# Storing half of one late output tile of a batched q·kᵀ through a second DMA queue (Trainium2, one core)

## The chip, the cores and the metric

The kernel runs on one core of a Trainium2 chip. The metric is device time in microseconds, here the median of three runs. Five engines run side by side: TensorE (PE), VectorE (DVE), ScalarE (ACT), GpSimd (POOL) and SyncE (SP). Copies between the chip's large memory and the cores' own memory are made by 16 DMA engines, which take their orders from queues; SP, ACT and POOL can each put copies on a queue of their own.

## The reference

Eight batches of twelve heads: for each of the 96 heads the 1024 x 1024 matrix of all dot products of a row of q with a row of k, in float32.

```python
batch, n_heads, seq, head_dim = 8, 12, 1024, 64
def reference(q, k):
    return np.einsum('bhid,bhjd->bhij', q, k).astype(np.float32)
```

The inputs are 25 MB each and the output is 403 MB.

## The kernel before, in words

The heads are worked on in blocks of 2, 2, 4, 8, 8 and then six times 12. For each block q and k are loaded as float32, cast to float16 by GpSimd (`cast_rows` L97, `cast_quads` L127), and transposed, by TensorE for the first two blocks (`transpose_rows` L151, L154) and by VectorE for the others (`transpose_quads` L145). The loads of a later block are issued from the ACT queue while an earlier block is being computed, the casts two blocks ahead, and the transposes one block ahead. The last loads are issued at about 734 us and the last cast begins at 831 us; after that the casts and loads are over and what is left is products and stores.

`scores` (L156 to L189) makes one head. TensorE fills a PSUM tile of two row groups with four products of 512 columns (L171), ScalarE copies the tile to a quarter of `o_sb` (L181), and this four times over. `o_sb` is one of three output buffers of 4 MB (`out_pool`, `bufs=3`): partition p holds the eight output rows 8p to 8p+7, 32 KB, which lie side by side in the output as well. When the four copies are done, SP issues one DMA of the whole head (L185), 128 partitions of 32 KB. So the copy of head n has to wait until the store of head n-3 has landed.

Everything is issued in program order (`pin`). SP's queue holds nothing but loads of the start and then the 96 stores in the order of the heads, each behind a wait for ScalarE's last copy. ACT's queue holds the loads. GpSimd issues no DMA. At the end (L304) SP waits until every DMA has landed.

Of the kernel before, what the change touches and what calls it, by code (L numbers as in the profile page):

```python
# [10 lines left out]
P = 128  # L11

@with_exitstack
def kernel(
# [6 lines left out]
    nc = tc.nc  # L21
# [3 lines left out]
    BH = B * H  # L25
# [5 lines left out]
    of = out.rearrange("b h i j -> (b h) i j")  # L31
# [4 lines left out]
    NMAX = max(sizes)  # L36
    CHUNK = 48 * 32

    consts = ctx.enter_context(tc.tile_pool(name="consts", bufs=1))
    ident = consts.tile([P, P], F16)  # L40

# [3 lines left out]
    out_pool = ctx.enter_context(tc.tile_pool(name="out_pool", bufs=3))  # L45

    pin = tc.keep_in_program_order

    def half_tile():
        half_sb = half_pool.tile([P, CHUNK], F16, tag="half")  # L50
        return half_sb

    class Block:
# [102 lines left out]
        def scores(self, n, side, ps_pool, w):  # L156

            half, g = divmod(n, self.N // 2)
            cs = slice(half * D, (half + 1) * D)

            qT = self.qT.rearrange("c (g m t) -> c g t m", t=NT, m=P)
            kT = self.kT.rearrange("c (g j) -> c g j", j=S)
            o_sb = out_pool.tile([P, NT, S], F32, tag="out")
            for u in range(NT // w):
                ps = ps_pool.tile([P, w * S], F32, tag="po")
                for tt in range(w):
                    for j in range(2):
                        js = slice(j * 512, (j + 1) * 512)
                        at = tt * S + j * 512
                        pin(  # L170
                            nc.tensor.matmul(  # L171
                                ps[:, at : at + 512],
                                qT[cs, g, w * u + tt],
                                kT[cs, g, js],
                            )
                        )
                dst = o_sb[:, w * u : w * u + w].rearrange("p t j -> p (t j)")
                if w == 1 and u % 2:
                    pin(nc.vector.tensor_copy(out=dst, in_=ps))  # L179
                else:  # L180
                    pin(nc.scalar.copy(out=dst, in_=ps))  # L181
                for do in side.get(u, []):
                    do()
            pin(
                nc.sync.dma_start(  # L185
                    out=of[self.first + n].rearrange("(p t) j -> p (t j)", p=P),
                    in_=o_sb.rearrange("p t j -> p (t j)"),
                )
            )  # L189

    blocks, first = [], 0
    for i, N in enumerate(sizes):
# [116 lines left out]
```

## Time and profile before

| what | value |
|---|---|
| median of three runs | 1063.12 us (1062.84 to 1063.62) |
| span of the profiled execution | 1061.8 us |
| what lies around it (median less span) | 1.3 us |
| busy: PE, ACT, DVE, POOL | 701.3, 697.6, 471.5, 368.3 us |
| stores on SP's queue q1 | 14688 packets, 406.85 MB, 89.1% of the 16 engines' span |
| loads on ACT's queue q10 | 2880 packets, 46.14 MB, 10.4% |
| mean DMA rate | 427 GB/s |
| issue of the last store, its landing | 1039.4 us, 1060.9 us |

The span runs from the first to the last instruction on the chip; the DMA share is the mean busy share of the 16 DMA engines, so that a share of 0.06 is one engine at work and fifteen idle. q1 includes the loads that SP issues at the start. The last twelve slices of the page show VectorE and GpSimd going idle one after the other, while the DMA row stays at 9 up to the last slice, which has a 7.

### The profile page before, as it was taken

The page shows a single profiled execution, that of the slowest core. Times are in us where ns is not written, and L with a number is a line of the kernel's source. Part 1 is how long each engine was busy: PE and PEld are TensorE (multiplying, and loading weights), DVE is VectorE, ACT ScalarE, POOL GpSimd, SP SyncE. Part 2 cuts the span into 40 slices and gives each one's busy share as a digit, 9 for nine tenths or more (in the row PEclk, how much of TensorE's full clock was granted, in tenths as well). Part 3 has the DMA queues.
Part 4 walks back from the last instruction along what each step waited for, and adds up shares of the span by engine and source line. Part 5 has one row for each costly group of instructions (what it writes and reads, how often), then busy time and mean ns, then how long its engine had stood idle before and what let it go on. Part 6 is the DMA issues. An engine that isn't in the chain of part 4 may idle for free.

```text
span 1061.8 us, 4282 instructions
## 1 busy us (share of the span) xinstructions
PE 701.3 (66%) x1568; PEld 241.6 (23%) x1568; DVE 471.5 (44%) x75; ACT 697.6 (66%) x386; POOL 368.3 (35%) x286
## 2 busy tenths in 40 slices
PE   6866755755677367773677836777367777778770
PEld 2322211211222122221222212222122222222220
DVE  2999601991696007960079600795007950000000
ACT  4856745755777366774677746777467777777771
POOL 6959128607630463303733046330463200000000
DMA  9999999999999999999999999999999999999997
GB/s 385 428 429 435 433 431 435 435 422 440 428 430 432 432 430 432 435 422 429 431 433 431 415 436 431 433 435 422 428 434 435 434 432 432 434 433 427 434 431 311
DMA packets 17588, 453.25 MB, mean 427 GB/s; under 512 B 1952, under 2 KB 1952, under 8 KB 2976
## 3 DMA queue, kind: packets, MB, share of 16 engines
q1 hardware_dynamic: 14688, 406.85, 89.1%
q10 hardware_dynamic: 2880, 46.14, 10.4%
q8 instruction: 12, 0.20, 0.1%
q14 instruction: 8, 0.07, 0.0%
HBM read 50.33 MB, written 402.65 MB: 427 GB/s over the span
## 4 chain that ended last, share of the span: by engine, by line
DMA 70%; ACT 17%; PE 7%; DVE 2%; issue 1%; POOL 1%; ACTq 0%; SPq 0%
DMA out_dram<-o_sb 70%; ACT o_sb L181 17%; PE ps L171 7%; DVE qT L145 1%; DVE kT L145 1%; DMA early<-in_q_dram 0%; POOL half_sb L127 0%; PE ps L151 0%; POOL half_sb L97 0%; DVE kT L154 0%; DVE o_sb L179 0%; ACTq L181 0%; ACT kT L154 0%; SPq L84 0%; ACTq L73 0%
## 5 line engine op out<-in xcount | busy, mean ns | idle before, releaser
L181 ACT COPY o_sb<-ps 128x2048 f32<-128x2048 f32 (+1 forms) x384 | 695.3, 1860 | 334.7 <-DMA out_dram<-o_sb 298.4
L171 PE MATMUL ps<-kT,qT 64*128 64x512 f16 x1536 | 697.2, 617 | 329.4 <-ACT o_sb L181 325.6
L127 POOL CAST half_sb<-x_sb 32x1536 f16<-32x1536 f32 (+1 forms) x256 | 346.5, 1353 | 455.1 <-DMA x_sb<-in_q_dram 318.3
L171 PEld LDWEIGHTS <-qT 64*128 64x128 f16 x1536 | 238.4, 157 | 786.3 <-issue 781.9
L145 DVE STREAM_TRANSPOSE qT<-half_sb 128x1536 f16<-128x1536 f16 (+1 forms) x34 | 232.8, 7140 | 372.2 <-issue 372.2
L145 DVE STREAM_TRANSPOSE kT<-half_sb 128x1536 f16<-128x1536 f16 (+1 forms) x34 | 234.2, 7181 | 0.0
L127 POOL CAST half_sb<-early 32x1024 f16<-32x1024 f32 x16 | 16.5, 1033 | 4.0 <-DMA early<-in_q_dram 3.3
L151 PE MATMUL ps<-ident,half_sb 128*128 128x128 f16 x32 | 4.1, 309 | 6.7 <-POOL half_sb L97 6.1
L154 DVE COPY qT<-ps 128x1024 f16<-128x1024 f16 x2 | 2.4, 1224 | 12.3 <-PE ps L151 12.3
L179 DVE COPY o_sb<-ps 128x1024 f32<-128x1024 f32 x4 | 4.9, 1224 | 4.3 <-PE ps L171 4.3
L97 POOL CAST half_sb<-early 128x512 f16<-128x512 f32 x8 | 4.6, 613 | 4.1 <-DMA early<-in_q_dram 4.1
L151 PEld LDWEIGHTS <-half_sb 128*128 128x128 f16 x32 | 3.2, 139 | 8.6 <-POOL half_sb L97 6.5
L154 ACT ACT_TABLE_LOAD x1 | 1.3, 1283 | 5.8 <-DMA early<-in_q_dram 5.8
L154 DVE COPY kT<-ps 128x1024 f16<-128x1024 f16 x1 | 1.2, 1224 | 4.3 <-PE ps L151 4.3
L154 ACT COPY kT<-ps 128x1024 f16<-128x1024 f16 x1 | 1.0, 1012 | 1.2 <-PE ps L151 1.2
masks.py:199 POOL TENSOR_SCALAR_AFFINE_SELECT ident<-ident 128x128 f16<-128x128 f16 x1 | 0.3, 292 | 0.1
masks.py:197 POOL MEMSET ident<- 128x128 f16 x1 | 0.2, 204 | 0.3 <-POOLq L293 0.3
L293 POOL MEMSET const-float32-0.0<- 128x1 f32 x1 | 0.1, 98 | 0.2 <-issue 0.2
L293 POOL MEMSET const-uint8-127<- 128x1 uint8 x1 | 0.1, 101 | 0.0
L293 POOL MEMSET const-bfloat16-1.0<- 128x1 bf16 x1 | 0.1, 100 | 0.0
L293 POOL MEMSET const-float32-1.0<- 128x1 f32 x1 | 0.1, 98 | 0.0
## 6 DMA issues: line engine op xcount, KB each, us to landing
out_dram<-o_sb SPq DMA_DIRECT2D x96, 4096.0 KB, 21.8
x_sb<-in_q_dram ACTq DMA_DIRECT2D x6, 3072.0 KB, 22.8
x_sb<-in_k_dram ACTq DMA_DIRECT2D x6, 3072.0 KB, 39.6
x_sb<-in_k_dram ACTq DMA_DIRECT2D x2, 2048.0 KB, 22.2
x_sb<-in_q_dram SPq DMA_DIRECT2D x1, 2048.0 KB, 18.0
x_sb<-in_q_dram ACTq DMA_DIRECT2D x1, 2048.0 KB, 19.0
early<-in_k_dram ACTq DMA_DIRECT2D x4, 256.0 KB, 5.0
early<-in_q_dram SPq DMA_DIRECT2D x4, 256.0 KB, 4.7
```

What stands on the lines that cost most here:

```text
L97: nc.gpsimd.tensor_copy(out=self.rows[x][:, :, half], in_=self.raw[x][:, half * n : (half + 1) * n].rearrange("p (r d) -> p r d", d=D),)
L127: nc.gpsimd.tensor_copy(out=half_sb[q0 : q0 + 32].rearrange("p (r d) -> p r d", d=32), in_=raw[32 * b : 32 * b + 32, c * m : (c + 1) * m, h],)
L145: pin(nc.vector.transpose(out=dst, in_=src))
L151: pin(nc.tensor.transpose(t_ps[:, t], self.rows[x][:, t], ident))
L154: pin(copy(out=dst, in_=src))
L171: nc.tensor.matmul(ps[:, at : at + 512], qT[cs, g, w * u + tt], kT[cs, g, js],)
L179: pin(nc.vector.tensor_copy(out=dst, in_=ps))
L181: pin(nc.scalar.copy(out=dst, in_=ps))
L293: nc = _bacc.Bacc("TRN2", target_bir_lowering=False, num_devices=1)
```

## The change

One head, the third from the end (head 93 of 0 to 95), is stored by four DMAs instead of one; the other 95 heads go as before. Each partition's eight rows are seen as two times two pairs of rows (a, b, t). The second pair of each four (b = 1) is stored by SP for all 128 partitions. The first pair of each four (b = 0) is stored by GpSimd for partitions 120 to 124 in one DMA, then by GpSimd for partitions 0 to 119 in a second one, and by SP for partitions 125 to 127. Every piece that is contiguous on both sides is 8 KB instead of 32 KB. The order of the issues in the program is: GpSimd 5, GpSimd 120, SP 128, SP 3. GpSimd's first issue waits for ScalarE's first three copies of the head by count (the fourth quarter holds rows 6 and 7, which are b = 1), and SP's for all four.

```diff
+    SPLIT = BH - 3
+    MOST = 120
+    SOME = MOST + 5
...
+    def store(eng, dst, src):
+        pin(eng.dma_start(out=dst, in_=src))
+
+    def store_head(head, dst, src):
+        if head != SPLIT:
+            store(
+                nc.sync,
+                dst.rearrange("p t j -> p (t j)"),
+                src.rearrange("p t j -> p (t j)"),
+            )
+            return
+        dst = dst.rearrange("p (a b t) j -> p a b (t j)", a=2, b=2)
+        src = src.rearrange("p (a b t) j -> p a b (t j)", a=2, b=2)
+
+        def part(eng, rows, b):
+            store(eng, dst[rows, :, b], src[rows, :, b])
+
+        part(nc.gpsimd, slice(MOST, SOME), 0)
+        part(nc.gpsimd, slice(0, MOST), 0)
+        part(nc.sync, slice(0, P), 1)
+        part(nc.sync, slice(SOME, P), 0)
...
-            pin(
-                nc.sync.dma_start(
-                    out=of[self.first + n].rearrange("(p t) j -> p (t j)", p=P),
-                    in_=o_sb.rearrange("p t j -> p (t j)"),
-                )
-            )
+            dst = of[self.first + n].rearrange("(p t) j -> p t j", p=P)
+            store_head(self.first + n, dst, o_sb)
```

## The prediction

> **What bounds the kernel now.** First the page: which resource is full, and when it stops being full.
>
> ```profile
> DMA  9999999999999999999999999999999999999997
> ...
> HBM read 50.33 MB, written 402.65 MB: 427 GB/s over the span
> ...
> DMA out_dram<-o_sb 70%; ACT o_sb L181 17%; PE ps L171 7%; DVE qT L145 1%; DVE kT L145 1%; DMA early<-in_q_dram 0%; POOL half_sb L127 0%; PE ps L151 0%; POOL half_sb L97 0%; DVE kT L154 0%; DVE o_sb L179 0%; ACTq L181 0%; ACT kT L154 0%; SPq L84 0%; ACTq L73 0%
> ...
> out_dram<-o_sb SPq DMA_DIRECT2D x96, 4096.0 KB, 21.8
> ```
>
> The DMA engines are full in every slice but the last, and the chain that ended last is mostly stores. Moving 453 MB cannot become cheaper by this change; only the last slice, where the engines are not full, can. So second, the stretches at the end (stretch, its length, busy time of the five engines, granted clock, DMA share, GB/s):
>
> ```profile
> 1050.00:1052.00 2.00, 0.00 (x0) 0.00 (x0) 0.00 (x0) 0.00 (x0) 0.00 (x0) 1.00 1.10 475
> 1052.00:1054.00 2.00, 0.00 (x0) 0.00 (x0) 0.00 (x0) 0.00 (x0) 0.00 (x0) 1.00 0.76 328
> 1054.00:1055.00 1.00, 0.00 (x0) 0.00 (x0) 0.00 (x0) 0.00 (x0) 0.00 (x0) 1.00 0.38 164
> 1055.00:1056.00 1.00, 0.00 (x0) 0.00 (x0) 0.00 (x0) 0.00 (x0) 0.00 (x0) 1.00 0.15 66
> 1056.00:1057.00 1.00, 0.00 (x0) 0.00 (x0) 0.00 (x0) 0.00 (x0) 0.00 (x0) 1.00 0.08 33
> 1057.00:1058.00 1.00, 0.00 (x0) 0.00 (x0) 0.00 (x0) 0.00 (x0) 0.00 (x0) 1.00 0.08 33
> 1058.00:1059.00 1.00, 0.00 (x0) 0.00 (x0) 0.00 (x0) 0.00 (x0) 0.00 (x0) 1.00 0.00 0
> 1059.00:1060.00 1.00, 0.00 (x0) 0.00 (x0) 0.00 (x0) 0.00 (x0) 0.00 (x0) 1.00 0.08 33
> ```
>
> A packet is counted where it starts. 33 GB/s in 1 us is one packet of 32 KB; it takes 1.213 us, which is 0.08 of sixteen engines for that us. From 1056 us on packets start one behind the other: **one engine alone works**, for about four packets, while fifteen are done. Nobody computes any more. Third, the packet and completion records of the trace, sorted by store. Each store is eight 32 KB packets and one increment on each of the 16 engines. The sixteen increments of the last store arrive, before the last one at 1060.9 us, by 8.0, 6.8, 6.5, 6.4, 6.3, 6.3, 6.3, 6.2, 5.9, 5.7, 5.6, 5.0, 4.7, 4.6 and 3.8 us. The gap between last and last but one is 0.3 us at the store that lands at 92 us, 2.3 at 460, 3.0 at 734 and 3.8 at the end: followed packet by packet, it is one engine whose packets take 1.213 to 1.231 us where the others' take 1.213, so 9.8 us for a store against 9.7. It sets the pace of the whole run and ends last. Fourth, the chain in order of time (start, us, what), and SP's own waits (total, times, longest):
>
> ```profile
> 1010.02 21.76 DMA out_dram<-o_sb
> ...
> 1031.88 1.87 ACT o_sb L181
> ```
>
> ```profile
> SPq L304 <- DMA out_dram<-o_sb: 21.0, 1, 21.0
> ```
>
> Three output buffers turn: head 95 (the last) may be written when head 92's store has landed at 1031.8, is copied by 1039.3 and issued at 1039.4. SP then waits 21.0 us for that store, until the late engine is done. That wait is all that the change can shorten.
>
> **The change, part by part.** Only head 93 (third from the end) is stored otherwise; its third copy ends at 1018.0 us, which frees GpSimd's part, and the fourth at 1019.8, which frees SP's.
>
> *Bytes on the engines.* Before, every engine moves 8 x 32 KB of head 93. After, half of it goes as before over all 128 partitions, as 16 packets of 8 KB to an engine. The other half is 120 + 5 + 3 partitions of 16 KB. At 8 partitions to an engine 120 is fifteen shares, so one engine gets none: it saves half a head, 4 x 1.213 = 4.85 us. The eight partitions left over go, one each, to up to five engines and to up to three: 2 packets of 8 KB = 2 x 0.309 = 0.62 us each (the 8 KB row is the instruction fetch, 0.309 us; 16 KB loads take 0.611), so 0, 0.62 or 1.24 us more on an engine. 8 KB packets instead of 32 KB: 0.309 x 4 = 1.236 against 1.213, 0.02 x 8 = 0.2 us on an engine at most. I take 0.1; nothing excludes a gain of 0.1, since later packets of the run vary between 1.213 and 1.23 anyway.
>
> *If the spared engine is the late one* it ends 4.85 earlier, or 4.85 - 0.62 = 4.2 if it has one of the five or three partitions: 1056.0 to 1056.7. Then the next in line is late. Last but one was at 1060.9 - 3.8 = 1057.1, the three before it at 1056.3, 1056.2 and 1055.9; with 0 to 1.24 more these end at 1057.1 to 1058.3, at 1057.5 at most, and so on. Eight extra shares lie on at most eight of the fifteen, so the engine at 1057.1 more likely has none; the others' worst is 1057.5. I take 1057.3 and 0.1 for small packets: 1057.4, that is **3.5 us** less (2.4 to 4.0).
>
> *The two GpSimd issues.* GpSimd's last cast ends at 832 us and it has nothing queued behind: its wait for ScalarE's third copy of head 93 holds up nobody. The trace shows no GpSimd issue. Bounds: 0.33 us (SP's store) to 1.26 us (the longest ACT load issue), below nothing excluded because it is a new instruction. Taken: 1 us each, hidden, since the transfer has until about 1056 us, 38 us after the third copy. If that cover were gone the part would land last, below.
>
> *SP's queue.* Two issues instead of one for head 93, 0.33 us each by the row, at most 1.26. Behind them stands head 94's issue at 1029.6; 9.8 us are free. Nothing.
>
> *Moving ahead.* A second queue means that GpSimd's half does not wait behind heads 91 and 92 on SP's queue. On fifteen engines up to 4.85 us of it may go ahead of head 92's packets; those engines were 4 to 8 us ahead of the late one, so head 92 still lands with the late one at 1031.8, at worst 4.85 later. Head 95 is then issued by 1044.3; the late engine would reach it at 1051.2 before. Cover 11.8 us from 1039.4, so nothing.
>
> *End.* SP waits on two more semaphores. The queue's rows show 0.2 to 0.4 us for such steps after the last landing: 0, since these two are up long before; at most 0.4.
>
> Sum on the profiled execution: 1061.8 - 3.5 = 1058.3. The median of the runs is 1063.12, 1.3 us above this span; taken over to the runs, 1063.1 - 3.5 = **1059.6 us**, 0.33% less.
>
> Which engine is spared decides all, and no view numbers the engines. [...] No trace here shows the numbers.
>
> **The rivals.**
>
> *Miss.* The engine left out is one of the fifteen punctual ones. Then the late engine keeps its half head and may get 0.62 or 1.24 us more, +0.1 for packets: 1060.9 + 0.1 to 1.3, in runs 1063.2 to 1064.4, **1063.6**. For it: nothing in the profile ties the late engine to the one left out; a blind draw would hit once in sixteen. Against: lateness belongs to one engine in all 96 stores, and a split by fixed counts leaves out a fixed engine, so it is hit in every run or in none, and the odds are those of a match of two fixed things. [...]
>
> *Not what it says.* GpSimd's 120 partitions are spread over all 16 engines evenly. The late engine then saves a sixteenth of half a head, 0.3 us: 1062.9 to 1063.4, within 0.2%.
>
> *Slower: head 95 waits for its buffer.* With two queues in flight stores took longer: the longest landing is 36.6 us against the median 21.8, 14.8 more, where loads stood on a second queue. If GpSimd's half delayed head 92 so, it would land at 1046.6, head 95 would be issued at 1054.2, past the 1051.2 where the late engine runs dry, and end 3 us later than before plus 1 to 2 us of start: 1066 to 1068, **1067**. It decides from a delay of 11.8 us. Against: those loads were 6 MB, GpSimd's part is 2 MB, 4.6 us at 432 GB/s.
>
> **How the numbers follow.** Hit 0.55, miss 0.34, evenly spread 0.04, slower by the buffer 0.07. The chance of a hit is a judgement: the sizes come from the trace, the match of the two engines does not; it is where I am least sure. Forecast 1059.6 with its own range 1059.0 to 1060.8. From 1058.8 to 1064.6 hit, miss and even spread are held, 0.9. A measurement of this kernel tells about 0.2% (2.1 us) from no change. Faster by more: the hit less its weakest end, 0.54. Within: 0.39. Slower: 0.07.
>
> **What would show it.** Right: in the last 6 us no stretch with one engine alone over 2 us; SP's last wait shorter than 21.0 by about 3.5; last landing near 1057.4; one engine with 4 packets of 32 KB less in the tail, and it is the late one. Miss: the row of single packets still there up to 1060 us or later, and the gap before the last increment 3 us or more. Slower: ScalarE's wait for the landing of head 92 longer than 2.3 us. Wrong sizes: 8 KB packets well over 0.31 us, or another engine made late by GpSimd's queue.

## The result, and the profile after

| | median us | runs | ratio to before, 95% interval |
|---|---|---|---|
| before, beside it | 1063.37 | 1062.84 to 1063.95 | |
| after | 1068.45 | 1068.12 to 1070.21 | 1.0053 [1.0038, 1.0067] |

The change makes the kernel 0.53% slower, about 5 us, where the prediction had 3.5 us less. The profiled execution after took 1068.75 us with a span of 1066.8 us, 5.0 more than the 1061.8 of before.

The page of after, first the two DMA rows of the slices, then the queues, the GpSimd line and the issues (out<-in, engine, count, KB each, median us from issue to landing):

```profile
DMA  9999999999999999999999999999999999999997
GB/s 378 431 432 434 432 426 430 432 431 431 434 433 424 430 435 430 434 426 431 432 431 432 424 432 433 432 432 426 429 435 432 432 434 432 431 434 431 429 354 314
...
q1 hardware_dynamic: 14825, 404.81, 88.5%
...
q0 software_dynamic: 320, 2.05, 0.7%
...
L54 POOL DMA_DIRECT2D out_dram<-o_sb x2 | 1.4, 714 | 186.2 <-ACT o_sb L207 186.2
...
out_dram<-o_sb SPq DMA_DIRECT2D x1, 2048.0 KB, 26.5
out_dram<-o_sb POOLq DMA_DIRECT2D x1, 1920.0 KB, 26.7
```

The row under the DMA row in the page of before:

```profile
GB/s 385 428 429 435 433 431 435 435 422 440 428 430 432 432 430 432 435 422 429 431 433 431 415 436 431 433 435 422 428 434 435 434 432 432 434 433 427 434 431 311
```

The DMA row reads as before: 9 in every slice but the last. The row under it doesn't: the last slice but one (1013 to 1040 us) moves 354 GB/s, where it moved 431 before and the ten slices ahead of it in after move 429 to 435. So the engines count as busy and carry less. The queue rows say the same: q0, GpSimd's, moves 2.05 MB of q1's 404.81, that is 0.51%, and takes 0.7% of the engines' span against q1's 88.5%, that is 0.79% of it.

The stretches of 4 us show where the 5 us go (stretch, length, busy time of the five engines, granted clock, DMA share, GB/s). First after:

```profile
1022.00:1026.00 4.00, 2.52 (x6) 0.94 (x6) 0.00 (x0) 3.82 (x3) 0.00 (x0) 1.00 1.02 354
1026.00:1030.00 4.00, 3.81 (x10) 1.39 (x9) 0.00 (x0) 3.02 (x2) 0.00 (x0) 1.00 0.98 307
1030.00:1034.00 4.00, 0.93 (x3) 0.20 (x2) 0.00 (x0) 0.00 (x0) 0.00 (x0) 1.00 0.93 283
1034.00:1038.00 4.00, 1.00 (x3) 0.46 (x3) 0.00 (x0) 2.92 (x2) 0.00 (x0) 1.00 0.99 311
1038.00:1042.00 4.00, 2.63 (x7) 0.63 (x4) 0.00 (x0) 3.82 (x3) 0.00 (x0) 1.00 1.05 371
```

The same stretches before:

```profile
1022.00:1026.00 4.00, 1.99 (x5) 0.78 (x5) 0.00 (x0) 3.73 (x3) 0.00 (x0) 1.00 1.01 434
1026.00:1030.00 4.00, 3.82 (x10) 1.27 (x9) 0.00 (x0) 3.56 (x2) 0.00 (x0) 1.00 1.03 442
1030.00:1034.00 4.00, 1.68 (x5) 0.62 (x4) 0.00 (x0) 2.12 (x2) 0.00 (x0) 1.00 0.99 426
1034.00:1038.00 4.00, 3.43 (x8) 0.95 (x6) 0.00 (x0) 3.83 (x3) 0.00 (x0) 1.00 1.03 442
1038.00:1042.00 4.00, 0.00 (x0) 0.00 (x0) 0.00 (x0) 1.33 (x1) 0.00 (x0) 1.00 0.93 401
```

The last column is the one to read. With a full rate of 432 GB/s (the mean from 940 to 980 us before, at a share of 1.00) the five stretches of after fall short by 78, 125, 149, 121 and 61 GB/s, 534 together; times 4 us and divided by 432 that is **4.9 us** of full transfer lost. The same sum for before is 0.1 us. So nearly the whole difference arises in these 20 us, while head 93's two halves are on the engines, at a share near 1.0 throughout. It is neither an idle engine nor one late engine: many packets take longer. By the packet records the 8 KB packets of GpSimd's queue take 458 ns in the mean and those of SP's queue 402, where 309 had been expected. Most still take about 309; 107 of GpSimd's 250 and 73 of SP's 262 take more than 330 ns, up to 2.4 us.

The tail of after, the stretches of 1 us:

```profile
1060.00:1061.00 1.00, 0.00 (x0) 0.00 (x0) 0.00 (x0) 0.00 (x0) 0.00 (x0) 1.00 0.23 98
1061.00:1062.00 1.00, 0.00 (x0) 0.00 (x0) 0.00 (x0) 0.00 (x0) 0.00 (x0) 1.00 0.23 98
1062.00:1063.00 1.00, 0.00 (x0) 0.00 (x0) 0.00 (x0) 0.00 (x0) 0.00 (x0) 1.00 0.08 33
1063.00:1064.00 1.00, 0.00 (x0) 0.00 (x0) 0.00 (x0) 0.00 (x0) 0.00 (x0) 1.00 0.08 33
```

The last increment comes at 1065.1, the one before 1.7 us earlier (3.8 before), the next 2.4. The part with one engine alone is shorter, as the forecast wanted, but it comes 5 us later. SP's last wait, in its list of waits, is accordingly longer and not shorter:

```profile
SPq L326 <- DMA out_dram<-o_sb: 22.2, 1, 22.2
```

### The profile page after: what moved, and what is told of

It reads as the page before. It is cut to its first block, busy times and chain, and to the rows that moved or that the text cites. A ratio compares the mean times of both kernels' runs of the same rounds, so it can differ in the third digit from the quotient of the medians.

```text
span 1066.8 us, 4286 instructions
## 1 busy us (share of the span) xinstructions
PE 701.0 (66%) x1568; PEld 241.6 (23%) x1568; DVE 471.5 (44%) x75; ACT 697.3 (65%) x386; POOL 369.8 (35%) x288
## 3 DMA queue, kind: packets, MB, share of 16 engines
q1 hardware_dynamic: 14825, 404.81, 88.5%
q0 software_dynamic: 320, 2.05, 0.7%
## 4 chain that ended last, share of the span: by engine, by line
DMA 70%; ACT 17%; PE 7%; DVE 2%; issue 1%; POOL 1%; ACTq 0%; SPq 0%
DMA out_dram<-o_sb 70%; ACT o_sb L207 17%; PE ps L197 7%; DVE qT L171 1%; DVE kT L171 1%; DMA early<-in_q_dram 0%; POOL half_sb L153 0%; PE ps L177 0%; POOL half_sb L123 0%; DVE kT L180 0%; DVE o_sb L205 0%; ACTq L207 0%; ACT kT L180 0%; SPq L110 0%; ACTq L99 0%
## 5 line engine op out<-in xcount | busy, mean ns | idle before, releaser
L54 POOL DMA_DIRECT2D out_dram<-o_sb x2 | 1.4, 714 | 186.2 <-ACT o_sb L207 186.2
```

The lines of the kernel that those rows point to most:

```text
L54: pin(eng.dma_start(out=dst, in_=src))
```

## The experiments

The letters in the expectations stand for the author's conjectures: A, that small packets are slow; B, that GpSimd's queue is slow by itself; C, that two queues taking turns on an engine cost time; D, that GpSimd's queue costs a fixed time per piece; E, that a store of fewer than 128 partitions makes several engines read partitions that share one way out of the on-chip memory. Where an edit names a part, it is one of the four `part(...)` lines of the change; what stands behind a `#` in the edits is put in here, and `...` stands for lines left out. "Lost" is worked out as above, from the stretches between 1022 and 1042 us against 432 GB/s, or those named.

| run | what it does with head 93 | median us | ratio [95%] | lost, us |
|---|---|---|---|---|
| after | 120 + 5 GpSimd, 128 + 3 SP, 8 KB | 1068.45 | 1.0053 [1.0038, 1.0067] | 4.9 |
| e1 | 128 + 128 SP, 8 KB | 1063.96 | 1.0005 [0.9996, 1.0015] | 0.0 |
| e2 | 128 GpSimd, 32 KB | 1065.54 | 1.0022 [1.0012, 1.0032] | see there |
| e3 | 128 ACT, 128 SP, 8 KB | 1063.53 | 1.0002 [0.9992, 1.0011] | 0.1 |
| e5 | 128 GpSimd, 128 SP, 8 KB | 1063.57 | 1.0004 [0.9995, 1.0013] | 0.0 |
| e6 | 5 + 120 + 128 + 3 SP, 8 KB | 1070.35 | 1.0062 [1.0047, 1.0077] | 4.8 |
| e7 | as after, 16 KB | 1068.32 | 1.0044 [1.0028, 1.0061] | 5.2 |
| e11 | 8 + 120 GpSimd, 128 SP, 8 KB | 1067.79 | 1.0044 [1.0029, 1.0059] | 4.9 |
| e12 | as after, on head 76 | 1067.39 | 1.0042 [1.0029, 1.0054] | 4.6 |
| e9 | as before, and partitions 32 to 95 once more | 1068.52 | 1.0049 [1.0034, 1.0064] | added bytes |
| e10 | as before, and partitions 0 to 63 once more | 1073.74 | 1.0104 [1.0088, 1.0121] | added bytes; 5.4 from 1034 to 1050 us |

### e1: small pieces alone

```diff
-        part(nc.gpsimd, slice(MOST, SOME), 0)
-        part(nc.gpsimd, slice(0, MOST), 0)
         part(nc.sync, slice(0, P), 1)
-        part(nc.sync, slice(SOME, P), 0)
+        part(nc.sync, slice(0, P), 0)
```

> Head 93 is cut into the same two halves of 8 KB pieces, but both are stored by SP, 128 partitions each; nothing goes by GpSimd and no engine is left out. Theory A (pieces of 8 KB are slow in themselves): the engines' rate falls to about 300 to 340 GB/s while head 93 is moved, about 4 to 5 us slower than before, 1067 to 1068 us. Theory B (GpSimd's queue is slow) and theory C (two queues that take turns on an engine in small pieces are slow): no dip beyond the 0.2 us that 32 packets of 309 ns cost against 8 of 1213 ns, 1063.1 to 1063.8 us.

1063.96 us, 0.2 above the range of theories B and C, but by its interval not to be told from before. All of head 93 goes in 8 KB packets, and these take 312 ns in the mean, the predicted row within 1%. No stretch falls below 408 GB/s; two of them:

```profile
1026.00:1030.00 4.00, 3.81 (x10) 1.43 (x9) 0.00 (x0) 2.97 (x2) 0.00 (x0) 1.00 0.97 408
1030.00:1034.00 4.00, 1.67 (x5) 0.47 (x3) 0.00 (x0) 2.70 (x2) 0.00 (x0) 1.00 1.00 420
```

Theory A falls, and nothing here speaks against the 0.1 us taken for packet size.

### e2: GpSimd's queue alone

```diff
-        dst = dst.rearrange("p (a b t) j -> p a b (t j)", a=2, b=2)
-        src = src.rearrange("p (a b t) j -> p a b (t j)", a=2, b=2)
...
-        part(nc.gpsimd, slice(MOST, SOME), 0)
-        part(nc.gpsimd, slice(0, MOST), 0)
-        part(nc.sync, slice(0, P), 1)
-        part(nc.sync, slice(SOME, P), 0)
+        dst = dst.rearrange("p t j -> p (t j)")
+        src = src.rearrange("p t j -> p (t j)")
...
+        part(nc.gpsimd, slice(0, P))    # 32 KB to a partition
```

> Head 93 is stored whole by GpSimd in one DMA of 128 partitions, 32 KB pieces; SP stores the other 95 heads. Theory B (GpSimd's queue is slow): a dip of the rate while the 4 MB are moved and 4 to 10 us more, 1067 to 1073 us. Theories A and C (small pieces, alone or in turns): packets stay at 1.21 to 1.23 us, the rate stays above 420 GB/s, 1063 to 1064 us; at most the wait of the last head's copy for its buffer grows, with 11.8 us of cover.

1065.54 us, 2.2 more than before and in the range of neither group of theories. The stretches of e2:

```profile
1026.00:1030.00 4.00, 3.81 (x10) 1.26 (x8) 0.00 (x0) 2.76 (x2) 0.00 (x0) 1.00 0.97 418
...
1034.00:1038.00 4.00, 0.00 (x0) 0.00 (x0) 0.00 (x0) 0.00 (x0) 0.00 (x0) 1.00 1.03 442
...
1042.00:1046.00 4.00, 0.42 (x2) 0.18 (x2) 0.00 (x0) 2.34 (x2) 0.00 (x0) 1.00 0.65 279
1046.00:1050.00 4.00, 3.21 (x8) 0.92 (x6) 0.00 (x0) 3.82 (x3) 0.00 (x0) 1.00 0.11 49
```

While GpSimd's 4 MB are on the engines, up to 1042 us, the rate is 418 to 442 GB/s, so the queue is not slow. Then the engines run dry, at 1042 to 1050, and ScalarE's timeline in e2 (start, us, instruction, idle before it and its releaser) says why:

```profile
1043.66 3.63 ACT L204 COPY o_sb<-ps 128x2048 f32<-128x2048 f32 x2 [14.90 <-DMA out_dram<-o_sb]
```

The last head's copies wait 14.90 us for a store: in this kernel its buffer is the one head 93 had, and the wait ends when GpSimd's store lands at 1043.6. Head 95 is issued at 1051.1, too late to keep the engines fed. That is a wait of the kind that the slower rival of the prediction has, the last head for its buffer, but for head 93's store instead of head 92's, and in a kernel that isn't the change.

### e3 and e5: two queues, each with 128 partitions

```diff
-        part(nc.gpsimd, slice(MOST, SOME), 0)
-        part(nc.gpsimd, slice(0, MOST), 0)
+        part(nc.scalar, slice(0, P), 0)      # e3
+        part(nc.gpsimd, slice(0, P), 0)      # e5
         part(nc.sync, slice(0, P), 1)
-        part(nc.sync, slice(SOME, P), 0)
```

> Head 93 in the same two halves of 8 KB pieces: one by SP, one by the ACT queue, 128 partitions each, both on hardware queues, no engine left out. Theory C (turns of two queues in small pieces): the rate dips to about 300 to 340 GB/s and it is 4 to 5 us slower, about 1068 us. Theory A: the same as C. Theory B (GpSimd's queue): no dip, 1063 to 1064 us.

> GpSimd stores its half of head 93 in one DMA of all 128 partitions (8 KB pieces), SP the other half; nothing is split by 120, 5 and 3. Theory D (GpSimd's queue pays a fixed 0.2 to 0.3 us for each 8 KB piece, which 32 KB pieces hide): the rate dips to about 300 GB/s as in the changed kernel, 1067 to 1068.5 us. Theory E (with 120 partitions on 15 engines the engines read other partitions than in a DMA of 128, two or three of them in the same group of partitions at once, and wait for each other): no dip, rate above 420 GB/s, 1063.2 to 1064 us.

1063.53 and 1063.57 us, both like before. e5 is the change with 128 partitions in place of 120 + 5 + 3 and nothing else. Its stretches and its queue row:

```profile
1026.00:1030.00 4.00, 3.81 (x9) 1.25 (x8) 0.00 (x0) 3.15 (x2) 0.00 (x0) 1.00 0.97 408
1030.00:1034.00 4.00, 1.06 (x3) 0.33 (x2) 0.00 (x0) 0.09 (x1) 0.00 (x0) 1.00 1.01 424
```

```profile
q0 software_dynamic: 272, 2.10, 0.5%
```

424 GB/s where after had 283, and q0 takes 0.5% of the engines' time for 2.10 MB, its due share; its packets take 312 ns. Theories B, C and D fall: neither GpSimd's queue nor two queues at once cost time here.

### e6: the odd split without GpSimd

```diff
-        part(nc.gpsimd, slice(MOST, SOME), 0)
-        part(nc.gpsimd, slice(0, MOST), 0)
+        part(nc.sync, slice(MOST, SOME), 0)
+        part(nc.sync, slice(0, MOST), 0)
```

> The four DMAs of the change, 5, 120, 128 and 3 partitions with 8 KB pieces, but all on SP's queue; GpSimd issues nothing. Theory D: no dip beyond 0.2 us, 1063 to 1064 us, or below if the engine left out is the late one. Theory E: the dip is back without GpSimd, rate about 300 GB/s while the 120 are moved, 1066 to 1069 us.

1070.35 us, 1.3 above the range of theory E: slower than before by as much as the change or a little more, with GpSimd issuing nothing. The 4.8 us lost do not make up all of it; what adds the rest isn't shown. Two stretches of e6:

```profile
1026.00:1030.00 4.00, 3.82 (x9) 1.26 (x8) 0.00 (x0) 3.60 (x2) 0.00 (x0) 1.00 0.95 276
1030.00:1034.00 4.00, 1.51 (x4) 0.48 (x3) 0.00 (x0) 0.00 (x0) 0.00 (x0) 1.00 0.99 287
```

Its 8 KB packets take 430 ns in the mean. e1 and e6 differ by the split of one half into 5, 120 and 3 partitions, and in the order of the halves; e5 and the change differ by the same split. The split is the cause.

### e7: larger pieces

```diff
-        dst = dst.rearrange("p (a b t) j -> p a b (t j)", a=2, b=2)
-        src = src.rearrange("p (a b t) j -> p a b (t j)", a=2, b=2)
+        dst = dst.rearrange("p (a b t) j -> p a b (t j)", a=1, b=2)
+        src = src.rearrange("p (a b t) j -> p a b (t j)", a=1, b=2)
```

> The change as it is, with GpSimd's 5 and 120 partitions and SP's 128 and 3, but each half is four rows side by side, so pieces of 16 KB instead of 8 KB. Theory D: half as many pieces, so half the loss or none, 1063.5 to 1065.8 us. Theory E: the engines share groups of partitions as before whatever the piece, the loss stays at 4 to 5 us, 1067 to 1069 us.

1068.32 us; 16 KB packets of 981 ns (GpSimd) and 737 ns (SP) against the 611 of before's loads. The loss is no smaller with half as many pieces (5.2 us against 4.9), so it goes by bytes, as E has it.

### e4 and e8: which engine is late

Both store heads 78, 82, 86 and 90 in several DMAs whose partition counts mark the engines, all by SP: 96+12+8+8+4, 96+14+10+6+2, 80+15+13+11+9 and 112+7+5+3+1. e4 stores the 32 KB of each partition that way; e8 stores all but the first 512 bytes of each partition in one DMA, and only those 512 bytes to a partition in the five. The edit from e4 to e8:

```diff
+        store(nc.sync, dst[:, TAIL:], src[:, TAIL:])      # TAIL = 128 float32
         at = 0
         for n in MARKS[head]:
-            part(nc.sync, slice(at, at + n))
+            store(nc.sync, dst[at : at + n, :TAIL], src[at : at + n, :TAIL])
             at += n
```

> Not a candidate: four heads (78, 82, 86, 90) are stored by SP in four or five DMAs of different numbers of partitions, 32 KB pieces, so that no two of the 16 engines get the same four packet counts if a DMA of k partitions with k up to 16 goes to the k lowest engines. Followed packet by packet, the engine with the slow packets (1.22 to 1.23 us) shows its number. [...] The time is about that of before plus 0 to 5 us, since counts differ by up to 4 packets of 1.21 us.

1121.85 us in one run, **58 us** more than before, where at most 5 had been expected. That miss gave theory E. Part of it is the uneven counts: an engine with a share of every small DMA has 40 packets of the four heads where the mean is 32, an estimate of 8 x 1.213 = 9.7 us. One stretch of e4:

```profile
876.00:896.00 20.00, 7.26 (x16) 2.52 (x16) 0.00 (x0) 8.32 (x5) 0.00 (x0) 1.00 1.01 305
```

Share 1.01 at 305 GB/s for 20 us. Of the 2428 packets of 32 KB after 870 us, 1913 take up to 1.25 us, 271 from there to 2.2, 166 from 2.2 to 2.6, and 78 longer, up to 14 us. The largest heap among the slow ones lies at 2.4 to 2.6 us, about twice 1.213, which is what two engines would need that share something with the rate of one; e4 alone doesn't show that they do. The order of the engines was too disturbed to read the marks.

> Not a candidate: heads 78, 82, 86 and 90 are stored by SP as 128 partitions without the first 512 bytes of each partition, and these 512 bytes in five DMAs of different numbers of partitions. If a DMA of k partitions up to 16 goes to the k lowest engines, each engine has its own count of 512-byte packets and the late engine, followed packet by packet, shows its number. With theory E the engines' order stays undisturbed since the odd DMAs are tiny, unlike in the run with 32 KB marks, whose packets took about 2.4 us, twice 1.21, wherever the split was uneven. Time 1063 to 1070 us.

1064.65 us in one run, and the order stays. Followed packet by packet, the late engine carried three of the marks at head 78 (12, 8 and 8, not the 4), three at head 82 (not the 2), four at head 86, two at head 90 (7 and 5, not the 3): a share of every mark of 5 or more partitions and of none of fewer. If a DMA of n partitions with n below 16 goes to the n lowest engines, as the expectation supposes, only number 4 fits; no run shows the number itself. Which engine the change spares, the trace of after shows without a number: the late engine carries two packets of GpSimd's 5-partition store, at 1022.19 and 1023.71, and after them only records of 4 bytes on that queue, so nothing of the 120 partitions. The change left out the engine that it was to leave out.

### e11: leave out another one

```diff
-    SOME = MOST + 5
+    SOME = MOST + 8
...
-        part(nc.sync, slice(SOME, P), 0)
```

> The change with 8 partitions in GpSimd's first DMA instead of 5 (none left for SP's last): if GpSimd's second DMA goes on from where the first stopped, it leaves out engine 7 instead of 4. Theory E: the loss to collisions stays. If leaving out the late engine (number 4 by the run with small marks) gained anything, this run is slower than the change by up to 4 us, 1069 to 1072 us; if a late group of partitions stays late whoever reads it, it is as the change, 1068 to 1069 us.

Which engine is left out here no view numbers; it is not the late one, which lands its part of the last head at 1064.0 us, last of all. 1067.79 us, 0.2 below both ranges and within the intervals the same as the change. Sparing the late engine was worth 3.5 us in the forecast; in the time of the kernel these runs can't tell it from sparing a punctual one.

### e12: the change 17 heads earlier

```diff
-    SPLIT = BH - 3
+    SPLIT = BH - 20
```

> The change on head 76 (at about 850 us, no loads under way) instead of head 93. Theory E: the engines lose 4 to 5 us for good, since they are full before and after, 1067 to 1068.5 us, and engine 4 has its lag again by the end or keeps what it was spared. A rival, that the loss comes from the end (the last head's buffer, landing and issue): no loss in the middle, 1063 to 1064 us.

1067.39 us. Stretches of e12, with computing in full swing:

```profile
860.00:864.00 4.00, 3.81 (x9) 1.10 (x7) 4.00 (x1) 3.16 (x2) 0.00 (x0) 1.00 1.01 320
864.00:868.00 4.00, 1.07 (x3) 0.33 (x2) 0.43 (x1) 0.00 (x0) 0.00 (x0) 1.00 0.98 322
```

From 856 to 880 us 4.6 us are lost, and nothing gives them back in the 200 us that follow. It is lost transfer time, not an effect of the last heads.

### e9 and e10: the partitions by themselves

The kernel before, and behind head 93's store one more store of 64 partitions of the same buffer, 32 KB each, to an unused tensor. This is added work of 2.1 MB, 4.85 us at 432 GB/s.

```diff
+    spare = nc.dram_tensor("spare", (64, NT * S), F32, kind="Internal").ap()
...
+            if self.first + n == BH - 3:
+                pin(
+                    nc.sync.dma_start(
+                        out=spare,
+                        in_=o_sb[32 : 96].rearrange("p t j -> p (t j)"),    # e10: o_sb[0 : 64]
+                    )
+                )
```

> The kernel before with one store more: behind head 93's store SP also copies partitions 32 to 95 of the same buffer, 64 pieces of 32 KB, to a scratch tensor in the large memory (the output is whole; 2.1 MB of work are added). That is 4 packets of 1.213 us on each engine, 4.85 us. [...] A rival, that any DMA of fewer than 128 partitions is slow: plus 9.7 us, 1073 us.

> The same with partitions 0 to 63: the same bytes, packets and engines. Theory E: two engines draw on each way out and half of the ways are idle, packets of 2.4 us, plus 8.5 to 10 us, 1072 to 1073.5 us. If partitions play no part (theory D and all others): as the run with partitions 32 to 95, 1068 to 1068.8 us.

Same bytes, same shape, same queue, same 16 engines; only the partitions differ. 1068.52 against 1073.74 us: 5.4 and **10.6** us above the 1063.12 beside them. e9, partitions 32 to 95:

```profile
1034.00:1038.00 4.00, 2.91 (x7) 0.78 (x5) 0.00 (x0) 3.82 (x3) 0.00 (x0) 1.00 1.01 434
1038.00:1042.00 4.00, 0.00 (x0) 0.00 (x0) 0.00 (x0) 0.81 (x1) 0.00 (x0) 1.00 1.03 442
1042.00:1046.00 4.00, 0.00 (x0) 0.00 (x0) 0.00 (x0) 0.00 (x0) 0.00 (x0) 1.00 0.97 418
```

e10, partitions 0 to 63:

```profile
1034.00:1038.00 4.00, 3.22 (x8) 0.93 (x6) 0.00 (x0) 3.82 (x3) 0.00 (x0) 1.00 1.01 287
1038.00:1042.00 4.00, 0.00 (x0) 0.00 (x0) 0.00 (x0) 1.12 (x1) 0.00 (x0) 1.00 1.09 246
1042.00:1046.00 4.00, 0.00 (x0) 0.00 (x0) 0.00 (x0) 0.00 (x0) 0.00 (x0) 1.00 0.87 246
```

The share is near 1.0 in both, the rate 418 to 442 in the one and 246 to 287 in the other. After 1022 us all 501 packets of 32 KB in e9 take 1.21 to 1.25 us; in e10, 45 of 498 take 2.2 us or longer. 64 partitions cost their bytes (4.85 expected, 5.4 measured) or twice their bytes (9.7 and 10.6), by which 64 they are. No letter but E lets the partitions matter; e10 came out 0.2 us above E's range. That two engines draw on each way out and half of the ways are idle, which that range rests on, no run shows; shown are the rate and the packet times above.

## Why the prediction was wrong

**The step that failed** is the one on the bytes on the engines, and in it the price of a packet: "8 KB packets instead of 32 KB: 0.309 x 4 = 1.236 against 1.213, 0.02 x 8 = 0.2 us on an engine at most". The size was not the trouble (e1: 312 ns). What failed was to carry a packet's time over to another split: the stores of before, and e1 and e5, have 128 partitions each. With 120 partitions on fifteen engines the same 8 KB take 402 to 458 ns in the mean, SP's half as well as GpSimd's, and 4.9 us are lost instead of 0.1 to 0.2. The prediction's last sentence on what would show it wrong, "8 KB packets well over 0.31 us, or another engine made late by GpSimd's queue", is what came, both halves, though not by the queue.

**What the slow packets hang on.** e9 and e10 show that the partitions decide: 2.1 MB from partitions 32 to 95 went at 418 to 442 GB/s, from 0 to 63 at 246 to 287. Which partitions belong together, and what the engines that read them share, no run shows; a shared way out is the author's conjecture, theory E. In size the loss of the change is like e10's, an estimate from the table: its 120 x 16 KB, 4.55 us at 432 GB/s, lost 4.9 us (after) and 4.6 to 5.2 (e6, e7, e11, e12), and e10's 64 x 32 KB, 4.85 us, lost 5.4. By that both took about twice the time of their bytes. But no run spreads 120 partitions over the engines in another way, so that the 120 are slow for e10's reason is argued. No view of before shows a doubling; with e10 at hand a rival could have stood in the prediction at 1063.1 + 4.5 = 1067.6 us.

**The late engine.** That one engine alone ends late, and that a split of 5 and then 120 leaves out just that one, was right (its packets in after). No view of before shows the fifteen shares or which engine they leave out, and the 0.55 for a hit was the author's judgement. What it was to save is there too. Followed packet by packet, the late engine lands its part of the last head at 1059.7 us in after, ahead of ten others; in e11, where it is not spared, it does so at 1064.0, last of all. These two traces are 4.3 us apart, where the prediction had 4.85 for half a head. The run doesn't get this, because the forecast had the next in line at 1057.1 to 1058.3, and in after the next in line are engines that the slow packets have held up: ten land after 1059.7, the last at 1065.1. That last one carried 36 of head 93's 8 KB packets, a share of each of the two small DMAs among them, where most carried 32.

The 3.8 us between the last engine and the next were also read from a single execution. In e1, e3 and e5, which spare no engine, they are 1.6, 2.9 and 1.4 us, so a spared engine could have gained less than 3.5 us even with packets of 0.31 us.

**The steps that held.** GpSimd's issues are off the path: two instructions of 714 ns behind a wait that nobody waits for (the L54 line above). SP's two issues took 0.68 and 1.35 us, the second over the bound of 1.26, and cost nothing: the next store was issued at 1029.0. Both the GpSimd half and SP's are landed by 1045.8 us, 19 us before the last landing. The last head's buffer did come later, and ScalarE's timeline in after shows the wait that the prediction named as the sign of the slower rival:

```profile
1035.08 3.63 ACT L207 COPY o_sb<-ps 128x2048 f32<-128x2048 f32 x2 [6.06 <-DMA out_dram<-o_sb]
```

6.06 us instead of 2.3, because head 92 landed at 1035.0, 3.2 us later than before. But head 95 was issued at 1042.6, when head 94's store still had 12.8 us to run (it landed at 1055.4), so the wait cost nothing; the cover of 11.8 us was not used up. That the slower rival's 1067 us lies close to the result is chance: the wait that it prices was there but did not decide. In e2 a wait of that kind did. No view of before shows the 1 to 2 us of start in that rival's sum; e2's last store, which found the engines dry, landed 11.1 us after its issue, 1.3 us more than the 9.8 us that the late engine takes for a store.

**What stays open.** Why one engine is slower (9.8 us for a store against 9.7), and its number, which is 4 only by what e8 supposes; whether it is the engine or the partitions that it reads; which engine reads which of the 120 partitions; and what a split would gain that spares the late engine without slow packets, which no run tried. No version tried beats the kernel before: e1, e3 and e5 lie within 0.05% of it, at or above it.

## What to carry to other kernels

A store that leaves one DMA engine free is not a store that costs the others nothing (4.9 us lost here): below 128 partitions, ask which partitions it reads, since the same 2.1 MB cost 5.4 us from partitions 32 to 95 and 10.6 us from 0 to 63. Look for a gap that one trace shows in a second trace before a forecast counts on it: here 3.8 us were 1.4 to 2.9 in others. Read GB/s beside the DMA share: a share near 1.0 at 246 to 310 GB/s, as here, hides packets that take longer while their engines count as busy. When a change alters the queue, the piece size and the split at once, vary each by itself; here two of the three were free.

## What the runs showed of the hardware

GpSimd's queue is as fast as SP's once it runs: 312 ns for 8 KB with 128 partitions (e5; SP's in e1 the same), the full 418 to 442 GB/s with 32 KB (e2). Its first packet came 4.4 us after the issue in after (1017.8 to 1022.2) and 5.0 in e2, while SP's stores filled the engines; that is not GpSimd's own, since ACT's queue took 4.7 us in e3 (1018.1 to 1022.8). And the loss lies in a part of the packets, not in all a little: in after 332 of head 93's 512 packets of 8 KB take at most 330 ns, the other 180 up to 2.4 us.
